# Where split weights and normed inputs begin in SBUF: four places 32 bytes apart, and two

## Chip, cores, metric

One core of one Trainium2 chip. The metric is the device time of one execution in microseconds (us), the median of several executions. Matmuls run on TensorE (PE), weight loads on the same engine's load path (PEld), and casts, sums and products on VectorE (DVE), ScalarE (ACT) and GpSimd (POOL).

## The reference, cut to what matters

Two layers run over 256 latent tokens and 256 context tokens, each 1,024 wide. A layer is a normed and modulated input, one wide input projection split among three token mixers (neighbourhood attention, retention, pooling), gated merges, an output projection and a SwiGLU feed-forward part:

```python
hx_n = _modulate(_rms_norm(h, norm1_g[l]), mx[:, 0], mx[:, 1])
hc_n = _modulate(_rms_norm(hc, norm1_g[l]), mc[0], mc[1])
mix_x, mix_c = _token_mixers(hx_n, hc_n, w_in[l], ...)
h = h + mx[:, 2] * mix_x
f_x = _modulate(_rms_norm(h, norm2_g[l]), mx[:, 3], mx[:, 4])
h = h + mx[:, 5] * _swiglu(f_x, w_ffn_gate[l], w_ffn_up[l], w_ffn_down[l])
```

In layer 0 the context tokens go the same way; in layer 1 they are only read. All in float32.

## The kernel before, in words

Every float32 product of a weight matrix is made of three matmuls on values cut in two. A value is rounded to the matmul's reduced float32 type (the high part) and the rest is kept as the low part; `mm3` (lines 194 to 198) then adds high by high (line 196), low weight by high input (197) and high weight by low input (198) into one PSUM bank.

The weights come in 276 chunks of 128 x 1024 floats, 138 a layer. For each chunk `load_to` issues the DMA into one of three `raw` tiles (line 99, SP's queue). `prep_to` takes one of four tiles with the tag `hl`, of 2 x 1024 floats a partition, and ACT casts the high half (line 124); `prep_lo` has DVE subtract for the low half (line 113). `use` keeps this three chunks ahead of the matmuls. In the trace the weight tiles and the low parts of the normed input have the same name, `hl`: in a matmul's row, the name behind the comma (`pg<-hh,hl`) is the stationary operand, the one before it is the moving operand.

The normed input `hn` is 8 pairs of tiles of 512 floats a partition: `hh` (high) and `hl` (low), 256 context columns and 256 latent columns each. It is written by the norm's modulation (`Mod`, lines 301 to 338) and, as the merged mixer output, by `msplit`. `fm` (line 209) walks chunks with the weights stationary and the input moving: 512 columns in layer 0, mostly 256 (the latent half) in layer 1. `tokmajor` (line 232) has it the other way round: the weights move, 512 columns at a time, and `hn` is stationary. The feed-forward part's second matrix reads `fh` and `fl` (line 1141), and the branch projections `naq` and `br`.

The order of the work is written out by hand; the program sets waits by the tile ranges that an instruction reads and writes. `edge` (line 1054) joins two stages in layer 0 and from layer 0 to 1; `edge1` (line 1117) joins the output projection and the feed-forward part in layer 1.

Tiles stand one behind the other in the order in which they are first asked for. In the program before, the four weight tiles begin at bytes 27,456, 35,648, 43,840 and 52,032 of a partition, the sixteen `hn` tiles at 68,416 and every 2,048 bytes from there, and the eleven pairs of `fh` and `fl` at 127,232 and every 2,048 from there. Modulo 128 that is 64 for all weights, 64 for all of `hn`, and 0 for `fh` and `fl`, and 0 for `naq` and `br` too.

Of the kernel before, what the change touches and what calls it, by code (L numbers as in the profile page):

```python
# [9 lines left out]
F32R = mybir.dt.float32r  # L10
# [8 lines left out]
KT = 8  # L19
# [13 lines left out]
def hybrid_dit_kernel(ctx: ExitStack, tc: tile.TileContext, hT, wst, adaf, adan, vec_d,  # L33
# [5 lines left out]
    wp = ctx.enter_context(tc.tile_pool(name="wp", bufs=1))  # L39
    act = ctx.enter_context(tc.tile_pool(name="act", bufs=1))  # L40
# [6 lines left out]
    def pg():  # L47
        return pbank("g", 4)
# [13 lines left out]
    def tiny(n, name="tiny"):  # L62
# [10 lines left out]
    mods = [con.tile([128, 48, 2], F32, name=f"mods{l}") for l in range(2)]  # L73
    Ag = [con.tile([128, 2, 8, 2], F32, name=f"Ag{l}") for l in range(2)]
    lg = [con.tile([128, 20], F32, name=f"lg{l}") for l in range(2)]
    hn = [(act.tile([128, 512], F32R, name=f"hh{k}"), act.tile([128, 512], F32R, name=f"hl{k}"))
          for k in range(KT)]
    h = []

    def h_tiles():  # L80
# [14 lines left out]
    def load_to(i):  # L95
        while st["dma"] <= min(i, total - 1):
            j = st["dma"]
            raw_t[j] = raw_tile()
            nc.sync.dma_start(out=raw_t[j], in_=wst[j])
            st["dma"] += 1  # L100

    late = []

    def parts(j, t):
        if j >= KT:
            return [(t, slice(0, 1024))]
        return [(t[:, :, :896], slice(0, 896)), (st["w7"][:, :, j], slice(896, 1024))]

    def prep_lo(i=total):
        while late and late[0][0] <= i:  # L110
            j, r, t = late.pop(0)
            for a, b in parts(j, t):
                V.tensor_tensor(a[:, 1], r[:, b], a[:, 0].bitcast(F32), op=ALU.subtract)  # L113

    def prep_to(i, wait=False):
        if not wait:
            prep_lo(i)
        while st["prep"] <= min(i, total - 1):
            j = st["prep"]
            load_to(j)  # L120
            t = wp.tile([128, 2, 1024], F32R, name="hl", tag="hl", bufs=4)
            r = raw_t.pop(j)
            for a, b in parts(j, t):
                S.copy(a[:, 0], r[:, b])  # L124
            late.append((j, r, t))
            if not wait:
                prep_lo(i)
            hl_t[j] = t
            st["prep"] += 1
# [7 lines left out]
    def use(i):  # L137
        prep_to(min(i + 3, st["cap"]), st["lazy"])
        load_to(i + 5)
        flush()  # L140
# [12 lines left out]
    def tick():  # L153
        step(lanes["pool"])
        step(lanes["rope"])
        step(lanes["attn"])
        if st["half"] == 0:
            prep_lo()
            st["credit"] += st["rate"]
            while ada_q and st["credit"] >= 1:  # L160
                ada_q.pop(0)()
                st["credit"] -= 1
        st["half"] ^= 1
# [7 lines left out]
    def ada_drain(n=0):  # L171
        while len(ada_q) > n:
            ada_q.pop(0)()
# [30 lines left out]
    def mmk(o, bl, xs, cols, k):  # L204
        n = cols.stop - cols.start
        hi, lo = xs[k]
        mm3(o[:, :n], blk(*bl[k]), (hi[:, cols], lo[:, cols]), k == 0, k == len(bl) - 1)

    def fm(specs, xs, cols, group=1):
        n = cols.stop - cols.start  # L210
        per = 2 if n == 512 else 4
        i = cnt = 0
        while i < len(specs):
            grp = specs[i:i + (group if i == 0 else 1)]
            i += len(grp)
            outs = [pg() for _ in grp]
            for k in range(len(grp[0][0])):
                for (bl, ev), o in zip(grp, outs):
                    if cnt % per == 0:
                        tick()  # L220
                    cnt += 1
                    prep_to(bl[k][0])
                    if (bl[k][1] == 4 or k == len(bl) // 2) and o is outs[0]:
                        use(bl[k][0])
                    mmk(o, bl, xs, cols, k)
            for (bl, ev), o in zip(grp, outs):
                ev(o[:, :n])

    def chunk8(j):
        return [(j, b) for b in range(8)]  # L230
# [57 lines left out]
    def norm_bcast(y, tiles, R):  # L288
        for i, t in enumerate(tiles):
            TE.matmul(R[:, t * 128:(t + 1) * 128], y[:, i:i + 1].to_broadcast([128, 128]), ident,  # L290
                      start=True, stop=True)
        return R
# [824 lines left out]
    def edge1(accs, l2, j2):  # L1117
        y = norm_rstd(norm_sum(accs, (2, 3)), 2)
        m = Mod(l2, j2, norm_bcast(y, (2, 3), pT()), (1,))
        return m  # L1120

    def out_ffn(l, fp):
        both = l == 0
        cq = ALL if both else X
        streams = (0, 1) if both else (1,)
        base = l * NCH
        acc = new_acc()
        last = [None]

        def ev_res(col, k, fin):  # L1130
            def ev(o):
                for s in streams:
                    residual(l, col, k, s, o[:, (CTX, X)[s]] if both else o)
                if fin and k < KT - 2:
                    defer.append(lambda: sq_acc(acc, k, cq))
                elif fin:
                    flush()
                    last[0] = sq_acc(acc, k, cq)
            return ev

        hid = [(fp.tile([128, 512], F32R, name=f"fh{j}"), fp.tile([128, 512], F32R, name=f"fl{j}"))
               for j in range(HALF)]

        def gate(o, e, c):
            if "s" not in e:
                e["s"] = fp.tile([128, 512], F32, name="sg", tag="sg", bufs=3)
            S.activation(e["s"][:, c], o, AF.Silu)  # L1147

        def upp(o, e, c, j):
            V.tensor_tensor(e["s"][:, c], o, e["s"][:, c], op=ALU.mult)  # L1150
            split([t[:, c] for t in hid[j]], e["s"][:, c])

        def gu(half, j0):
            c0 = base + CF + half * 33
            specs = []
            for j in range(j0, HALF):
                e = {}
                specs += [(chunk8(c0 + 2 * j), lambda o, e=e: gate(o, e, cq)),
                          (chunk8(c0 + 2 * j + 1), lambda o, e=e, j=j: upp(o, e, cq, j))]
            return specs  # L1160

        sqrt_table()
        wo = [chunk8(base + CO + k) for k in range(KT)]
        specs = [(wo[k], ev_res(16, k, True)) for k in range(KT)]
        heads = [chunk8(base + CF + i) for i in range(3)]
        if both:
            ada_drain(16)
            st["rate"] = 0.0
            fm(specs[:6], hn, cq, group=2)
            outs = edge(wo[6:], hn, 16, l, acc, heads, l, 1)  # L1170
            ada_units(1, (0, 1), (0, 1))
            ada_units(1, (2, 3, 4, 5), (1,))
            st["rate"] = 0.6
            specs = gu(0, 0)
            for (_, ev), o in zip(specs, outs):
                ev(o)
            fm(specs[3:], hn, cq)
        else:
            ada_drain()
            st["cap"] = base + CF + 1  # L1180
            fm(specs, hn, cq, group=2)
            edge1((acc, last[0]), l, 1).go(8)
            st["cap"] = 10 ** 6
            fm(gu(0, 0), hn, cq, group=2)

        def down(half):
            c1 = base + CF + half * 33 + 22
            return [[(c1 + (11 * k + q) // 8, (11 * k + q) % 8) for q in range(11)] for k in range(KT)]

        if both:  # L1190
            ada_drain(64)
        fm([(bl, ev_res(40, k, False)) for k, bl in enumerate(down(0))], hid, cq)
        fm(gu(1, 0), hn, cq)
        sqrt_table()
        acc = new_acc()
        dn = down(1)
        specs = [(bl, ev_res(40, k, True)) for k, bl in enumerate(dn)]
        if both:
            st["rate"] = 0.0
            fm(specs[:6], hid, cq)  # L1200
            ada_drain(32)
            return edge(dn[6:], hid, 40, l, acc, [chunk8(NCH + CK + i) for i in range(3)], 1, 0)
        fm(specs[:7], hid, cq)
        yt = fp.tile([128, KT, 256], F32, name="yt")

        def scaled(k):
            S.activation(yt[:, k], h[k][:, X], AF.Copy, scale=vec[:, V_FG + k:V_FG + k + 1])

        for k in range(KT - 1):
            scaled(k)  # L1210
        fm(specs[7:], hid, cq)
        o = norm_sum((acc, last[0]), (2, 3))
        scaled(KT - 1)
        y = norm_rstd(o, 2)
        R = norm_bcast(y, (2, 3), pT())
        for k in range(KT):
            V.tensor_tensor(yt[:, k], yt[:, k], R[:, X], op=ALU.mult)
            if k % 2:
                nc.sync.dma_start(out=out[:, k - 1:k + 1], in_=yt[:, k - 1:k + 1])
# [130 lines left out]
```

## Time and profile before

| | before |
|---|---|
| median of 3 runs | 1366.77 us (1366.04 to 1368.06) |
| the profiled execution's own time | 1367.57 us |
| its span, first to last instruction | 1365.8 us |
| PE busy | 1326.2 us, 97% |
| DVE, ACT, POOL busy | 847.6, 580.7, 152.7 us |
| mean granted TensorE clock | 0.987 of full speed |

The span is what the trace shows; the profiled execution's time is 1.8 us longer than it. Matmuls are pipelined: the time that one takes from its start to its end is longer than the distance to the start of the next, so a matmul's cost in a dense stretch is read as the distance of starts.

### The profile page before, as it was taken

Reading aid. Unit: us, or ns where it says so; the run is one execution under the profiler, and the core shown is the slowest. Engines: PE = TensorE matmul, PEld = TensorE weight load, DVE = VectorE, ACT = ScalarE, POOL = GpSimd, SP = SyncE. Lnnn points to the kernel's source line nnn. Section 1 sums busy time; section 2 is a strip of 40 time slices with the busy share of each in tenths; the row PEclk is TensorE's granted clock in tenths of the full one; section 3 lists DMA queues with packets and bytes.
Section 4 is the critical chain, followed back from the end, with each engine's and each line's share of the span. In section 5 each row is a group of like instructions: output and inputs, shape, how many; then the busy total and the mean of one; then the engine's idle time right before and its main releaser. Section 6 shows DMA issues by size and latency. Waiting matters only on the chain.

```text
span 1365.8 us, 20012 instructions
## 1 busy us (share of the span) xinstructions
PE 1326.2 (97%) x7842; PEld 1151.9 (84%) x7842; DVE 847.6 (62%) x1454; ACT 580.7 (43%) x907; POOL 152.7 (11%) x213
## 2 busy tenths in 40 slices
PE   7999999899999999999999999999999999999997
PEld 5777777788888898888888888988889999899997
DVE  4566452877877666566565654676438877655554
ACT  4455555452232444232123232456466545643453
POOL 0034113211000010000000000232134200000000
PEclk8999999999999999999999999999999999999998
DMA  8433312343544514454445652143336665455552
GB/s 301 164 99 132 104 63 92 124 137 126 169 170 163 192 62 154 139 170 158 149 140 186 212 171 87 61 159 108 131 124 197 223 239 185 140 185 198 181 176 95
DMA packets 61150, 207.28 MB, mean 152 GB/s; under 512 B 6912, under 2 KB 11392, under 8 KB 60032
## 3 DMA queue, kind: packets, MB, share of 16 engines
q1 hardware_dynamic: 49392, 163.96, 35.8%
q10 hardware_dynamic: 11664, 42.04, 9.1%
q8 instruction: 62, 1.02, 0.3%
q14 instruction: 32, 0.26, 0.1%
HBM read 204.93 MB, written 1.05 MB: 151 GB/s over the span
## 4 chain that ended last, share of the span: by engine, by line
PE 89%; DVE 6%; ACT 3%; issue 1%; DMA 1%; POOL 0%; DVEq 0%; ACTq 0%; SPq 0%; POOLq 0%
PE pg L196 26%; PE pg L197 26%; PE pg L198 26%; PE po L941 1%; PE po L687 1%; PE pt L675 1%; DVE hl L113 1%; PE po L459 1%; PE ps L643 1%; PE ps L644 1%; DVE nakl L628 1%; DMA bm<-in_bias 1%; DVE rkl L876 0%; DVE naq L638 0%; DVE acc L494 0%
## 5 line engine op out<-in xcount | busy, mean ns | idle before, releaser
L196 PE MATMUL pg<-hh,hl 128*128 128x256 f32 (+1 forms) x1568 | 528.1, 337 | 2.5 <-ACT tmp L1000 1.4
L197 PE MATMUL pg<-hh,hl 128*128 128x256 f32 (+1 forms) x1568 | 522.9, 333 | 1.4 <-DVE hl L113 1.4
L198 PE MATMUL pg<-hl,hl 128*128 128x256 f32 (+1 forms) x1568 | 523.3, 334 | 0.6 <-POOL hl L326 0.5
L113 DVE TENSOR_TENSOR hl<-raw,hl 128x1024 fp32r<-128x1024 f32 (+1 forms) x276 | 341.4, 1241 | 172.2 <-ACT hl L124 166.9
L124 ACT CAST hl<-raw 128x1024 fp32r<-128x1024 f32 (+1 forms) x276 | 286.9, 1043 | 211.4 <-PE pg L198 112.3
L196 PEld LDWEIGHTS pg<-hh,hl 128*128 128x128 f32 x1568 | 299.7, 191 | 36.1 <-issue 3.8
L197 PEld LDWEIGHTS pg<-hh,hl 128*128 128x128 f32 x1568 | 299.6, 191 | 31.1 <-DVE hl L113 2.1
L198 PEld LDWEIGHTS pg<-hl,hl 128*128 128x128 f32 x1568 | 299.2, 191 | 30.6 <-POOL hl L326 1.4
L385 DVE CUSTOM_DVE_ANT_0 tmp<-ada,cb 128x1024 bf16<-128x1024 f32 x128 | 156.1, 1226 | 26.7 <-DMA ada<-in_adaf 17.3
L196 PE MATMUL pg<-fh,hl 128*128 128x256 f32 (+1 forms) x374 | 121.6, 325 | 0.0
L197 PE MATMUL pg<-fh,hl 128*128 128x256 f32 (+1 forms) x374 | 121.4, 325 | 0.0
L198 PE MATMUL pg<-fl,hl 128*128 128x256 f32 (+1 forms) x374 | 121.4, 325 | 0.0
L326 POOL TENSOR_TENSOR hl<-tmp,hh 128x256 fp32r<-128x256 f32 x20 | 14.8, 739 | 626.3 <-ACT hh L315 371.1
L298 ACT CAST fh<-sg 128x512 fp32r<-128x512 f32 (+1 forms) x44 | 22.6, 513 | 141.0 <-DVE sg L1150 141.0
L196 PEld LDWEIGHTS pg<-fh,hl 128*128 128x128 f32 x374 | 70.1, 187 | 7.2
L198 PEld LDWEIGHTS pg<-fl,hl 128*128 128x128 f32 x374 | 70.1, 187 | 7.2
L197 PEld LDWEIGHTS pg<-fh,hl 128*128 128x128 f32 x374 | 70.1, 188 | 7.1
L342 DVE SCALAR_TENSOR_TENSOR h<-pg,mods,h 128x256 f32<-128x256 f32 x72 | 32.7, 479 | 65.6 <-PE pg L198 65.4
L1150 DVE TENSOR_TENSOR sg<-pg,sg 128x512 f32<-128x512 f32 (+1 forms) x44 | 24.5, 556 | 51.2 <-PE pg L198 47.8
L1000 ACT ACTIVATE tmp<-pg 128x512 f32<-128x512 f32 (+1 forms) x48 | 23.5, 490 | 76.4 <-PE pg L198 75.2
L196 PE MATMUL pg<-hl,hh 128*128 128x512 f32 x128 | 50.8, 397 | 1.7 <-DVE nakl L628 1.7
L1147 ACT ACTIVATE sg<-pg 128x512 f32<-128x512 f32 (+1 forms) x44 | 21.6, 490 | 68.4 <-PE pg L198 68.4
(248 smaller groups left out, 1555.7 us busy)
## 6 DMA issues: line engine op xcount, KB each, us to landing
raw<-in_wst SPq DMA_DIRECT2D x276, 512.0 KB, 3.8
ada<-in_adaf ACTq DMA_DIRECT2D x80, 512.0 KB, 4.2
wn<-in_adan SPq DMA_DIRECT2D x8, 1024.0 KB, 7.4
h<-in_hT SPq DMA_DIRECT2D x16, 256.0 KB, 5.5
bm<-in_bias SPq DMA_DIRECT2D x32, 128.0 KB, 2.1
out<-yt SPq DMA_DIRECT2D x4, 256.0 KB, 3.2
cs<-in_rope SPq DMA_DIRECT2D x2, 256.0 KB, 3.1
pw<-in_pw SPq DMA_DIRECT2D x2, 256.0 KB, 3.8
```

The lines of the kernel that those rows point to most:

```text
L113: V.tensor_tensor(a[:, 1], r[:, b], a[:, 0].bitcast(F32), op=ALU.subtract)
L124: S.copy(a[:, 0], r[:, b])
L196: TE.matmul(o, wh, xh, start=a, stop=False)
L197: TE.matmul(o, wl, xh, start=False, stop=False)
L198: TE.matmul(o, wh, xl, start=False, stop=z)
L298: S.copy(d0, src)
L326: P.tensor_tensor(hn[k][1][:, c], t[:, c], hi, op=ALU.subtract)
L342: V.scalar_tensor_tensor(h[k][:, c], o, mods[l][:, col + k, s:s + 1], h[k][:, c], op0=ALU.mult, op1=ALU.add)
L385: V.tensor_tensor_reduce(out=tmp().bitcast(BF16), in0=tiles[n], in1=cb[s], scale=1.0, scalar=0.0, op0=ALU.mult, op1=ALU.add, accum_out=mod ...
L1000: S.activation(sg[f][:, cl], o, AF.Sigmoid)
L1147: S.activation(e["s"][:, c], o, AF.Silu)
L1150: V.tensor_tensor(e["s"][:, c], o, e["s"][:, c], op=ALU.mult)
```

## The change

The sixteen `hn` tiles become one tile of 16 x 512 + 32 floats, and `hn_at(off)` sets the sixteen views to begin `off` floats into it: 0 at first, 16 floats (64 bytes) from just ahead of the modulation that makes layer 1's mixer input, and 0 again from just ahead of the one that makes layer 1's feed-forward input. The four weight tiles become one tile of 4 x 2048 + 32 floats, in which chunk j takes the 2048 floats from `2048 * (j % 4) + 8 * (j % 4)`: each of the four places begins 32 bytes further into its 8,192 than the one before. This tile is asked for ahead of `raw`, and so stands ahead of it.

```diff
-    hn = [(act.tile([128, 512], F32R, name=f"hh{k}"), act.tile([128, 512], F32R, name=f"hl{k}"))
-          for k in range(KT)]
+    hnb = act.tile([128, 16 * 512 + 32], F32R, name="hn")
+    hn = []
+
+    def hn_at(off):
+        v = [hnb[:, 512 * i + off:512 * i + off + 512] for i in range(16)]
+        hn[:] = [(v[2 * k], v[2 * k + 1]) for k in range(KT)]
+
+    hn_at(0)
...
+    hlb = wp.tile([128, 4 * 2048 + 32], F32R, name="hl")
...
-            t = wp.tile([128, 2, 1024], F32R, name="hl", tag="hl", bufs=4)
+            t = hlb
+            o = 2048 * (j % 4) + 8 * (j % 4)
+            t = t[:, o:o + 2048].rearrange("p (a n) -> p a n", a=2)
...
             fm(specs, hn, cq, group=2)
+            hn_at(0)
             edge1((acc, last[0]), l, 1).go(8)
...
             ada_drain(32)
+            hn_at(16)
             return edge(dn[6:], hid, 40, l, acc, [chunk8(NCH + CK + i) for i in range(3)], 1, 0)
```

## Rows read from the trace of the kernel before

**Rows 1.** The page: busy time of PE; the chain's shares by engine.

```profile
PE 1326.2 (97%) x7842; PEld 1151.9 (84%) x7842; DVE 847.6 (62%) x1454; ACT 580.7 (43%) x907; POOL 152.7 (11%) x213
...
PE 89%; DVE 6%; ACT 3%; issue 1%; DMA 1%; POOL 0%; DVEq 0%; ACTq 0%; SPq 0%; POOLq 0%
```

**Rows 2.** Groups by line and form on PE: count, busy us, mean ns, idle before.

```profile
L196 PE MATMUL pg<-hh,hl 128*128 128x512 f32 x720 | 285.2, 396 | 0.0
...
L196 PE MATMUL pg<-hh,hl 128*128 128x256 f32 x848 | 242.9, 286 | 2.5 <-ACT tmp L1000 1.4 <-ACT hh L317 1.1
...
L196 PE MATMUL pg<-fh,hl 128*128 128x256 f32 x220 | 61.0, 277 | 0.0
...
L196 PE MATMUL pg<-fh,hl 128*128 128x512 f32 x154 | 60.7, 394 | 0.0
...
L196 PE MATMUL pg<-hl,hh 128*128 128x512 f32 x128 | 50.8, 397 | 1.7 <-DVE nakl L628 1.7
...
L196 PE MATMUL pg<-br,hl 128*128 128x512 f32 x64 | 25.4, 397 | 0.0
```

**Rows 3.** Windows on PE: stretch, length, busy (instructions), granted clock, DMA share, GB/s.

```profile
520.00:620.00 100.00, 100.00 (x443) 1.00 0.47 158
...
1170.00:1230.00 60.00, 60.00 (x503) 1.00 0.57 186
```

**Rows 4.** Timeline of PE (start us, us, instruction): ends of four dense stretches.

```profile
599.86 0.39 PE L198 MATMUL pg<-hl,hl 128*128 128x512 f32 x1
...
605.98 0.39 PE L198 MATMUL pg<-hl,hl 128*128 128x512 f32 x1
...
679.95 0.39 PE L196 MATMUL pg<-fh,hl 128*128 128x512 f32 x1
...
682.98 0.39 PE L197 MATMUL pg<-fh,hl 128*128 128x512 f32 x1
...
1199.73 0.28 PE L198 MATMUL pg<-hl,hl 128*128 128x256 f32 x1
...
1200.57 0.28 PE L196 MATMUL pg<-hh,hl 128*128 128x256 f32 x1
...
1249.78 0.28 PE L198 MATMUL pg<-fl,hl 128*128 128x256 f32 x1
...
1250.57 0.28 PE L196 MATMUL pg<-fh,hl 128*128 128x256 f32 x1
```

**Rows 5.** Groups by line and form on PE, from 864.5 to 1166 us.

```profile
L196 PE MATMUL pg<-hh,hl 128*128 128x256 f32 x416 | 119.4, 287 | 1.4 <-ACT tmp L1000 1.4
...
L197 PE MATMUL pg<-hh,hl 128*128 128x512 f32 x24 | 9.4, 392 | 0.0
```

**Rows 6.** Timeline of PE where two attention matmuls cut into a dense stretch.

```profile
102.06 0.39 PE L196 MATMUL pg<-hl,hh 128*128 128x512 f32 x1
...
102.52 0.39 PE L198 MATMUL pg<-hl,hh 128*128 128x512 f32 x1
102.74 0.39 PE L643 MATMUL ps<-nakd,naq 128*128 128x512 f32 x1
102.97 0.39 PE L644 MATMUL ps<-nakl,naq 128*128 128x512 f32 x1
...
104.12 0.39 PE L197 MATMUL pg<-hl,hl 128*128 128x512 f32 x1
```

**Rows 7.** The page's groups for the split's two steps, and PE's longest waits for it.

```profile
L113 DVE TENSOR_TENSOR hl<-raw,hl 128x1024 fp32r<-128x1024 f32 (+1 forms) x276 | 341.4, 1241 | 172.2 <-ACT hl L124 166.9
L124 ACT CAST hl<-raw 128x1024 fp32r<-128x1024 f32 (+1 forms) x276 | 286.9, 1043 | 211.4 <-PE pg L198 112.3
...
PE pg L197 <- DVE hl L113: 1.4, 3, 0.9
```

**Rows 8.** Timeline of the kernel's end: products into one tile, its DMAs out.

```profile
1358.95 2.73 DVE L1217 TENSOR_TENSOR yt<-yt,pt 128x256 f32<-128x256 f32 x8 [1.38 <-PE pt L290]
1359.79 2.59 SPq L1219 DMA_DIRECT2D out<-yt  x4
```

## The prediction, made before the changed kernel was run

> **What bounds the kernel now.** I read the page first: PE is busy for 97% of the span and the chain that ended last is 89% PE [rows 1]. So the time is the number of matmuls times the distance between their starts, and little else. The groups by line and form come next: lines 196 to 198 have one group each for every moving tile and width, nearly without idle time before them [rows 2]. The reader should see the counts there; each stands for one of the three lines of `mm3`. The windows then show that two dense stretches run at a granted clock of 1.00, the upper of its two levels (2.4 GHz) [rows 3], so what follows is not the clock. Last the timeline, for the distance of starts in four dense stretches [rows 4]:
>
> - `hn` moving, 512 columns: 599.86 to 605.98 us, 27 distances, 226.7 ns each.
> - `fh` moving, 512 columns: 679.95 to 682.98, 13 distances, 233.1 ns.
> - `hn` moving, 256 columns: 1199.73 to 1200.57, 7 distances, 120.0 ns.
> - `fh` moving, 256 columns: 1249.78 to 1250.57, 7 distances, 112.9 ns, with a rounding of some 1 ns.
>
> These four rates are the case. The weights come from the same four tiles in all of them; what differs is the moving tile. `hn` and the weights begin at 64 modulo 128, `fh` at 0. With `hn`, 512 columns are 6.5 ns cheaper than with `fh`, and 256 columns 7 ns dearer. So a start place does carry a price in this kernel, of about 6.7 ns a matmul, with a sign that turns with the width. If a column took one cycle of 2.4 GHz (an estimate: 213.3 and 106.7 ns for 512 and 256 columns), the excess would be 13 or 20 ns at the one width and 13 or 6.5 at the other: whole steps of 6.7.
>
> **What the change does, part by part.** Instructions: none are added or removed. ACT still casts 276 chunks, DVE still subtracts, SP still issues one load each, and the loads land in `raw` as before. The order on every queue stays.
>
> Places: the weight block is now asked for ahead of `raw`, so it takes byte 15,168 (27,456 less the three `raw` tiles of 4,096), and its four places begin at 64, 96, 0 and 32 modulo 128. `hn` moves to 68,544 (128 bytes on, for the 32 extra floats), which is 64 modulo 128 with offset 0 as before, and 0 with offset 16. Everything behind it moves by 256 bytes, so `fh`, `naq` and `br` stay at 0.
>
> Reading A, my forecast: the place of the moving operand sets the rate. That is how the rows differ, and in one more place: where a matmul on 64-placed data is followed by one whose weights are `naq`, at 0, its distance is 102.52 to 102.74, 0.22 us, no dearer than its neighbours [rows 6]. Then only these change:
>
> - `hn` at offset 16, 256 columns: 416 a line between 864.5 and 1166 us [rows 5], times three lines, 1,248 matmuls. From 120.0 to 113.3: 1,248 x 6.7 ns = -8.3 us.
> - `hn` at offset 16, 512 columns (keys and the retention's keys, which read the context too): 24 a line, 72 matmuls [rows 5], from 226.7 to 233.3: +0.5 us.
> - `tokmajor`, where the weights move: 128 a line, 384 matmuls [rows 2], a quarter at each place. At 64 nothing; at 0, 96 x 6.7 = +0.6 us; at 32 and 96 no row shows a price, so bounds: nothing, or one step of 6.7 on 192, +1.3 us. I take half, +0.6.
>
> Sum: -8.3 + 0.5 + 0.6 + 0.6 = -6.6 us.
>
> The 32-byte starts of the stationary operand are the largest unknown. Nothing in the trace of before loads weights for these matmuls from a place that is not a multiple of 64. The nearest rows are the two rates of each width [rows 4]. From below: half of all matmuls go from the dearer rate to the cheaper. From above: half go from the cheaper to the dearer. Beyond that by one further step of 6.7 ns on that half, either way. I take nothing, since by reading A the stationary place has no price, and keep both ends for the range.
>
> Rule and row: the Trainium skill's page "TensorE: Matmul & The Clock Gate", section "Part 2: What happens when you issue a matmul", says that the engine has two independent SBUF read ports, so that loading the next weights takes nothing from the running matmul. By that rule no place of either operand would matter, all groups would have one rate a width, and the sum would be 0 instead of -6.6 us. The rows disagree: 226.7 against 233.1 at 512 columns, 120.0 against 112.9 at 256.
>
> The split: ACT's cast takes 1,043 ns and DVE's subtraction 1,241 ns a chunk [rows 7], 2.3 us together, written to other start places than before. PE waited for DVE's low half three times, 1.4 us in all [rows 7], because the split runs three chunks ahead (24 matmuls of 120 to 227 ns each, 2.9 to 5.4 us a chunk). I cost a dearer write at nothing. If the cover were gone, a chunk in layer 1 would have to take over 2.9 us on DVE alone; 1,241 ns is far off.
>
> Waits: both blocks are now one tile each. The four weight ranges don't overlap (each begins 2,056 floats behind the last), so a cast waits for the last reader of the same place, as before for the tile of four chunks ago. `hn` at offset 16 overlaps its neighbour's old range by 64 bytes, but a modulation writes only after the sums over outputs that are made behind the last reads of the old `hn`. Cost nothing. If the program instead waited by whole tiles, every chunk would show its 2.3 us of split to PE: 276 x 2.3 = 630 us. Against that: DVE's 8 products into `yt` run without a break from 1358.95 while DMAs read other slices of the same tile from 1359.79 [rows 8].
>
> **The rivals.**
>
> B, the difference of the two places sets the rate. Before, it is 0 with `hn` and 64 with `fh`. After, every stage takes all four differences in turn, and the two that rows show average to 230.0 and 116.7 ns. 512 columns: 720 x 3 with `hn` and 384 in `tokmajor`, +3.3 ns each, +8.5 us; `fh` 154 x 3, -3.3, -1.5 us. 256 columns: 848 x 3 with `hn`, -8.5 us; `fh` 220 x 3, +2.2 us. The branch tiles have as many matmuls at either width and cancel (one row, x64, stands for them [rows 2]). Sum +0.7 us: no change, 1368. For it: from 102.06 to 104.12 nine distances take 2.06 us, 20 ns over nine of 226.7 [rows 6], and three of these matmuls have operands 64 apart: three steps of 6.7, where A has one. Against it: the step into `naq` itself is not dearer.
>
> C, a start at 32 or 96 takes the dearer rate at both widths: half of 2,544 matmuls of 512 columns with `hn` or moving weights, +6.7 ns, +8.5 us; half of some 950 at 256 columns with `fh` and the branch tiles, +3.2 us. Sum +11.7, 1379 us: slower. With A's gain beside it +5, still slower; it outweighs A from 2 ns on half of all 6,800 or so matmuls. One step beyond the dearer rate on that half would be 23 us more, 1402.
>
> D, a start at 32 or 96 takes the cheaper rate at both widths: half of 2,544 at 256 columns with `hn`, -8.5 us; half of some 750 at 512 with `fh` and the branches, -2.5. Sum -11, 1357 us; with one step beyond it, 1334.
>
> E, no place matters and the rates belong to the tiles for another reason, as the port rule above would have it: 1367 us.
>
> W, waits by whole tiles: about 2000 us.
>
> **How the numbers follow.** The sum goes against the profiled execution's own time: 1367.6 - 6.6 = 1361.0 us. The median shown lies 0.8 us lower, so I predict 1360.2. Chances: A 0.34, D 0.14, B and E together 0.23, C 0.27, W 0.02. What a measurement of this kernel can tell from no change is about 0.2%, 2.7 us. Faster: A and D, 0.48. Same: B and E, 0.23. Slower: C and W, 0.29. The range reaches from most of D to C's 1379: 1348 to 1380. Left out are the further steps on either side, and W, some 0.17. A's own range is 1357 to 1364 (its weakest term, the moving weights, and a tenth of the gain lost where a stretch of layer 1 is broken up by attention matmuls).
>
> **What would show it.** The profile after should have, in layer 1's gates and output projection, distances of 113 ns where there were 120; in layer 0's feed-forward stretch all at 226.7, whichever chunk; in layer 1's feed-forward part 120 still. Alternation from chunk to chunk, every 24 matmuls, would show that the stationary place counts, and refute A for B, C or D by the rates that the four chunks have. Waits of PE for `hl` beyond the 1.4 us would point to the split or to W. The prediction is wrong if weights at 32 or 96 have a rate that no row of before shows, or if the rate turns with a period other than 128 bytes, which these rows can't tell.

## The result: 1379.16 us, 0.9% slower, and the profile after

The kernel after takes 1379.16 us (1378.5 to 1382.1, three runs) beside 1366.77 us before: a ratio of 1.0090, 95% interval 1.0074 to 1.0106. The forecast was 1360.2. The profiled execution took 1378.5 us with a span of 1376.6; its granted clock is 0.987, as before.

The page after, the engines' busy time, which answers to [rows 1], and the split's two steps and PE's wait for it, which answer to [rows 7] (the wait with its total us, count and longest):

```profile
PE 1338.6 (97%) x7842; PEld 1153.7 (84%) x7842; DVE 848.4 (62%) x1454; ACT 580.6 (42%) x907; POOL 151.5 (11%) x213
...
L120 DVE TENSOR_TENSOR hl<-raw,hl 128x1024 fp32r<-128x1024 f32 (+1 forms) x276 | 341.6, 1242 | 176.9 <-ACT hl L133 174.9
L133 ACT CAST hl<-raw 128x1024 fp32r<-128x1024 f32 (+1 forms) x276 | 286.7, 1042 | 211.8 <-PE pg L207 110.8
...
PE pg L206 <- DVE hl L120: 0.8, 3, 0.3
```

As many instructions as before, DVE and ACT as busy as before, the subtraction and the cast as long to 1 ns, and PE waits for a low half three times, 0.8 us in all. Only PE is busier, 1338.6 us against 1326.2. So 12.4 us went into the matmuls themselves: into the distance between their starts.

Where along the span, the timeline tells. Three places in the kernel before (the first matmul of 256 columns at the end of layer 0's feed-forward part, the first down product of layer 1, the last product of all), and the same three after (lines 205 to 207 are 196 to 198 moved on):

```profile
849.35 0.28 PE L196 MATMUL pg<-fh,hl 128*128 128x256 f32 x1
...
1231.17 0.29 PE L196 MATMUL pg<-fh,hl 128*128 128x256 f32 x1
...
1354.28 0.28 PE L198 MATMUL pg<-fl,hl 128*128 128x256 f32 x1
```

```profile
859.10 0.28 PE L205 MATMUL pg<-fh,hl 128*128 128x256 f32 x1
...
1240.55 0.28 PE L205 MATMUL pg<-fh,hl 128*128 128x256 f32 x1
...
1365.41 0.29 PE L207 MATMUL pg<-fl,hl 128*128 128x256 f32 x1
```

The kernel after is 9.75 us late at the first, 9.38 at the second, 11.13 at the third. Nearly all of the loss is in layer 0, where the matmuls have 512 columns. From the first place to the second lie layer 1's mixer, from which the forecast took 8.3 us, and the first gate and up projections: together they gave back 0.4.

The timeline of after in two dense stretches, the first matmul of each chunk (24 matmuls from one to the next): `hn` with 512 columns and `fh` with 256. They answer to [rows 4].

```profile
695.94 0.40 PE L205 MATMUL pg<-hn,hl 128*128 128x512 f32 x1
...
701.44 0.40 PE L205 MATMUL pg<-hn,hl 128*128 128x512 f32 x1
...
707.04 0.40 PE L205 MATMUL pg<-hn,hl 128*128 128x512 f32 x1
...
712.62 0.39 PE L205 MATMUL pg<-hn,hl 128*128 128x512 f32 x1
...
718.23 0.40 PE L205 MATMUL pg<-hn,hl 128*128 128x512 f32 x1
...
1243.28 0.28 PE L205 MATMUL pg<-fh,hl 128*128 128x256 f32 x1
...
1246.16 0.28 PE L205 MATMUL pg<-fh,hl 128*128 128x256 f32 x1
...
1249.01 0.28 PE L205 MATMUL pg<-fh,hl 128*128 128x256 f32 x1
...
1251.88 0.30 PE L205 MATMUL pg<-fh,hl 128*128 128x256 f32 x1
...
1254.64 0.28 PE L205 MATMUL pg<-fh,hl 128*128 128x256 f32 x1
```

With 512 columns four chunks take 5.50, 5.60, 5.58 and 5.61 us: 229, 233, 232.5 and 234 ns a matmul, 232.2 on the mean, where before had 226.7 in its dense stretch. With `fh` and 256 columns they take 2.88, 2.85, 2.87 and 2.76 us: 120, 119, 119.5 and 115 ns, where before had 112.9. The rate turns from chunk to chunk, which the prediction named as what would refute reading A.

The windows of after, `hn` with 512 columns and `hn` at its first place with 256 (the columns are those of [rows 3], with the busy time of PE, PEld, DVE, ACT and POOL ahead of the clock):

```profile
700.00:800.00 100.00, 100.00 (x432) 80.90 (x432) 57.52 (x81) 28.29 (x36) 0.00 (x0) 1.00 0.55 184
...
1275.00:1325.00 50.00, 50.00 (x424) 50.00 (x423) 28.55 (x36) 23.83 (x36) 0.00 (x0) 1.00 0.54 186
```

The granted clock stands at 1.00, its upper level, in both: the clock is not the cause. 424 matmuls in 50 us, of which two overlap the ends, are 118.5 ns each at the second, where before had 120.0.

### The profile page after: what moved, and what is told of

It reads as the page before. It is cut to its first block, busy times and chain, and to the rows that moved or that the text cites. A ratio compares the mean times of both kernels' runs of the same rounds, so it can differ in the third digit from the quotient of the medians.

```text
span 1376.6 us, 20011 instructions
## 1 busy us (share of the span) xinstructions
PE 1338.6 (97%) x7842; PEld 1153.7 (84%) x7842; DVE 848.4 (62%) x1454; ACT 580.6 (42%) x907; POOL 151.5 (11%) x213
## 4 chain that ended last, share of the span: by engine, by line
PE 93%; DVE 3%; ACT 2%; issue 1%; DMA 0%; SPq 0%; POOL 0%; ACTq 0%; DVEq 0%; POOLq 0%
PE pg L205 28%; PE pg L206 28%; PE pg L207 28%; PE po L950 1%; PE po L696 1%; PE pt L684 1%; PE po L468 1%; PE ps L653 1%; PE ps L652 1%; DVE hl L120 1%; DMA h<-in_hT 0%; PE pg L789 0%; ACT hl L133 0%; ACT hn L326 0%; PE ps L922 0%
## 5 line engine op out<-in xcount | busy, mean ns | idle before, releaser
L205 PE MATMUL pg<-hn,hl 128*128 128x256 f32 (+1 forms) x1568 | 530.1, 338 | 2.5 <-ACT tmp L1009 1.4
L206 PE MATMUL pg<-hn,hl 128*128 128x256 f32 (+1 forms) x1568 | 524.3, 334 | 0.8 <-DVE hl L120 0.8
L207 PE MATMUL pg<-hn,hl 128*128 128x256 f32 (+1 forms) x1568 | 524.3, 334 | 0.5 <-POOL hn L335 0.4
L205 PEld LDWEIGHTS pg<-hn,hl 128*128 128x128 f32 x1568 | 297.1, 189 | 39.6 <-issue 3.6
L206 PEld LDWEIGHTS pg<-hn,hl 128*128 128x128 f32 x1568 | 297.1, 189 | 33.8 <-DVE hl L120 1.5
L207 PEld LDWEIGHTS pg<-hn,hl 128*128 128x128 f32 x1568 | 296.8, 189 | 33.5 <-POOL hn L335 1.3
L335 POOL TENSOR_TENSOR hn<-tmp,hn 128x256 fp32r<-128x256 f32 x20 | 14.8, 738 | 634.4 <-ACT hn L324 372.6
L205 PE MATMUL pg<-hl,hn 128*128 128x512 f32 x128 | 51.3, 401 | 1.7 <-DVE nakl L637 1.7
```

The source lines that it names most:

```text
L205: TE.matmul(o, wh, xh, start=a, stop=False)
L206: TE.matmul(o, wl, xh, start=False, stop=False)
L207: TE.matmul(o, wh, xl, start=False, stop=z)
L335: P.tensor_tensor(hn[k][1][:, c], t[:, c], hi, op=ALU.subtract)
```

## The experiments

**The theories.** In what follows, the distance is one of addresses: the start of the weights less the start of the moving operand, modulo 256 bytes. The time from the start of one matmul to that of the next is given in ns, as the matmul's rate. From the start places that the prediction and the list of tiles give: before, it is 0 with `hn` and 64 with the hidden tiles `fh`, in all chunks. After, the weights stand at 64, 96, 128 and 160 modulo 256, `hn` at 192 (its first place) and 0 (its second), `fh` at 0; so it is 128, 160, 192 and 224 with `hn` at its first place, and 64, 96, 128 and 160 with `hn` at its second and with `fh`.

- Theory 1: this distance sets the rate.
- Theory 2: starts 32 bytes off a 64-byte step are dear (rival C).
- Theory 3: the moving operand's place alone counts (reading A, which takes it modulo 128).
- Theory 4: merging the tiles costs the time by itself.

Each edit below is against the kernel after. Times stand beside those of before on the same chip.

**One place.** The merged tiles stay, the places go back.

```
-    hnb = act.tile([128, 16 * 512 + 32], F32R, name="hn")
+    hnb = act.tile([128, 16 * 512 + 96], F32R, name="hn")
...
-    hn_at(0)
+    hn_at(32)
...
-            o = 2048 * (j % 4) + 8 * (j % 4)
+            o = 2048 * (j % 4)
...
-            hn_at(0)
...
-            hn_at(16)
```

> The two large tiles of the change stay, but every weight chunk begins at the same place in its 8,192 bytes and the normed input has one place, so that each stationary operand starts as far from its moving operand, counted modulo 256 bytes, as in the kernel before: 0 bytes for the normed input, 64 for the FFN's hidden tiles. Theory 1 (the rate of the matmuls follows the distance between the start of the weights and the start of the moving operand, modulo 256): all four rates of [rows 4] come back, 226.7 and 233.1 ns at 512 columns, 120.0 and 112.9 at 256, and the time is that of before, 1,365 to 1,369 us. Theory 4 (merging sixteen and four tiles into one each, with the order of writes and waits that follows, costs the time): the distances of the kernel after stay, and so does most of its 12 us: 1,375 to 1,380 us.

1367.69 us, ratio 0.9992 (0.9982 to 1.0001). Its window from 700 to 800 us has 443 matmuls where after has 432; 100 us by 226.7 ns are 441. Merging costs nothing: theory 4 falls, and what the change costs, the places cost.

**Weights at one place, `hn` at two.**

```
-            o = 2048 * (j % 4) + 8 * (j % 4)
+            o = 2048 * (j % 4)
```

> The normed input has its two places as in the change; the weights have one, so no start is 32 bytes off a 64-byte step. Theory 1 (distance of the two starts modulo 256): normed input at its first place 128 bytes apart, at its second 64. Layer 0, 512 columns: 232.4 ns in every chunk (as after shows for its first of four places) where before has 226.7; layer-1 mixer at 256 columns 113.3 in every chunk where before has 120.0; layer-1 FFN 118.7; the hidden tiles as before. Sum against before: 2,160 x 5.7 ns = +12.3, about 1,240 x -6.7 = -8.3, about 1,290 x -1.3 = -1.7, and +1.6 for the token-major products: +4 us, 1,369 to 1,373 us. Theory 2 (starts 32 bytes off a 64-byte step cost, as rival C of the prediction has it): none is left, so nothing above before: 1,367 us or less. Theory 3 (the moving operand's place alone, reading A): layer 0 stays at 226.7, the layer-1 mixer goes to 113, about 1,360 us.

1372.78 us, ratio 1.0035 (1.0022 to 1.0049), +4.2 us where theory 1 said +4. Its window, the first product of 256 columns at the end of layer 0's feed-forward part, and a stretch of 48 matmuls of layer 1's mixer (the last line is the first matmul behind them):

```profile
700.00:800.00 100.00, 100.00 (x432) 81.08 (x431) 57.50 (x81) 28.30 (x36) 0.00 (x0) 1.00 0.57 182
...
858.17 0.28 PE L205 MATMUL pg<-fh,hl 128*128 128x256 f32 x1
...
1128.02 0.28 PE L205 MATMUL pg<-hn,hl 128*128 128x256 f32 x1
...
1133.46 0.28 PE L205 MATMUL pg<-br,hl 128*128 128x256 f32 x1
```

432 matmuls in 100 us, as in after, though no start is 32 bytes off: theory 2 falls. And `hn` stands at 64 modulo 128 here as it did before, with the weights at one place as before, and yet takes 232 ns where it took 226.7: reading A falls, and the period is not 128 bytes. That the place of the moving operand counts alone, but modulo 256, this run does not exclude; the next one does. At 858.17 us this kernel is 8.82 us behind the kernel before, where after is 9.75 behind: nearly all of layer 0's loss is here with the weights at one place. It comes from the 128 bytes by which the padding moved `hn`. The mixer's stretch takes 5.44 us, 113.3 ns each, as distance 64 should.

**Four places, `hn` moved to suit.** The weights keep the change's places; `hn` goes 128 bytes on, to distances of 0, 32, 64 and 96.

```
-    hnb = act.tile([128, 16 * 512 + 32], F32R, name="hn")
+    hnb = act.tile([128, 16 * 512 + 64], F32R, name="hn")
...
-    hn_at(0)
+    hn_at(32)
...
-            hn_at(0)
...
-            hn_at(16)
```

> The weights keep the change's four places 32 bytes apart; the normed input has one place throughout, so that the distances to it are 0, 32, 64 and 96 bytes in turn, and to the hidden tiles 192, 224, 0 and 32. Theory 1 (distance modulo 256): with 512 columns the first of four chunks takes 226.7 ns, the third and fourth 233.3; with 256 columns the first 120.0, the third 113.3, the fourth 120.0; the second, at 32 bytes, was not seen before and lies between 226.7 and 233.3, and 113 and 120. Hidden tiles: 229, 233, 226.7, unknown at 512, and 118, 118, 120, unknown at 256. Against after: 2,160 x -0.3 to -2.0 ns, 2,540 x -1.6 to +0.1 ns: 0 to -8 us, 1,371 to 1,379 us. Theory 2 (starts 32 bytes off a 64-byte step cost): the second and fourth of four chunks dear, the first and third cheap, in both widths the same chunks. Theory 3 (the moving operand's place alone): no alternation from chunk to chunk.

1378.39 us, ratio 1.0070 (1.0055 to 1.0085). The timeline, four chunks of `hn` with 512 columns and four with 256:

```profile
687.63 0.40 PE L205 MATMUL pg<-hn,hl 128*128 128x512 f32 x1
...
693.23 0.40 PE L205 MATMUL pg<-hn,hl 128*128 128x512 f32 x1
...
698.82 0.39 PE L205 MATMUL pg<-hn,hl 128*128 128x512 f32 x1
...
704.44 0.39 PE L205 MATMUL pg<-hn,hl 128*128 128x512 f32 x1
...
709.91 0.39 PE L205 MATMUL pg<-hn,hl 128*128 128x512 f32 x1
...
1273.59 0.28 PE L205 MATMUL pg<-hn,hl 128*128 128x256 f32 x1
...
1276.45 0.28 PE L205 MATMUL pg<-hn,hl 128*128 128x256 f32 x1
...
1279.29 0.28 PE L205 MATMUL pg<-hn,hl 128*128 128x256 f32 x1
...
1282.12 0.28 PE L205 MATMUL pg<-hn,hl 128*128 128x256 f32 x1
...
1284.93 0.28 PE L205 MATMUL pg<-hn,hl 128*128 128x256 f32 x1
```

At 512 columns the distances 32, 64, 96 and 0 take 233, 233, 234 and 228 ns: theory 1 to 1.3 ns. `hn` begins at one place in all four, so its place alone, modulo whatever number, does not set the rate: theory 3 falls altogether. At 256 columns the distances 0, 32, 64 and 96 take 119, 118, 118 and 117 ns, where 120, a new value, 113.3 and 120 were expected: here the theory gives the size only to some 5 ns. The last experiment, which finds 113.3 and 117.7 ns at distance 64, accounts for the third value, not for the fourth: at 256 columns, where the distance turns from chunk to chunk, it does not settle the rate alone.

**Two distances, chosen.** One place for the weights; distance 0 for `hn` and the hidden tiles of layer 0 (512 columns), 64 throughout layer 1 (256 columns).

```
-    hnb = act.tile([128, 16 * 512 + 32], F32R, name="hn")
+    hnb = act.tile([128, 16 * 512 + 64], F32R, name="hn")
...
-    hlb = wp.tile([128, 4 * 2048 + 32], F32R, name="hl")
+    hlb = wp.tile([128, 4 * 2048], F32R, name="hl")
...
-            o = 2048 * (j % 4) + 8 * (j % 4)
+            o = 2048 * (j % 4)
...
-            hn_at(0)
...
-            hn_at(16)
+            hn_at(48)
...
         with tc.tile_pool(name="ff0", bufs=1) as fp:
+            P.memset(fp.tile([128, 16], F32, name="pad"), 0.0)
```

> One place for the weights; the moving operands placed so that with 512 columns the two starts are 0 bytes apart modulo 256 (the normed input and the hidden tiles of layer 0) and in layer 1, at 256 columns, 64 bytes apart. Theory 1: 512 columns at 226.7 ns for the hidden tiles too (462 x -6.4 ns = -3.0 us against before), 256 columns at 113.3 for the normed input of layer 1 (about 2,286 x -6.7 = -15.2), some +1.8 for the 256-column products with the hidden tiles of layer 0 and the token-major products of layer 1: -16.5 us, 1,348 to 1,354 us. Theory 3 (the moving operand's place alone) expects the same of this kernel. Theory 2 (only starts 32 bytes off cost): no difference to before, 1,367 us.

1355.56 us, ratio 0.9923 (0.9891 to 0.9956): faster than both kernels, though short of the 1,348 to 1,354 expected, and its six times spread from 1350.0 to 1363.9. Its windows, `hn` and `fh` with 512 columns, `hn` and `fh` with 256:

```profile
700.00:800.00 100.00, 100.00 (x443) 82.81 (x442) 59.72 (x85) 29.19 (x37) 0.00 (x0) 1.00 0.60 196
640.00:690.00 50.00, 50.00 (x223) 41.38 (x222) 27.78 (x46) 9.96 (x10) 0.00 (x0) 1.00 0.47 152
1275.00:1325.00 50.00, 50.00 (x444) 50.00 (x443) 30.14 (x39) 25.95 (x38) 0.00 (x0) 1.00 0.58 193
```

443, 223 and 444 matmuls; after has 432 and 424 in the first and third, and 216 in the second. These are the rates of distances 0 and 64: the hidden tiles of layer 0 now run like `hn`, and `hn` of layer 1 as `fh` did.

**One column 128 times.** After, with the second FFN half's gate and up projections fed from one column of each weight block.

```
     def blk(j, b):
         t = hl_t[j]
+        if st.get("one"):
+            return [t[:, i, b * 128:b * 128 + 1].to_broadcast([128, 128]) for i in range(2)]
         return t[:, 0, b * 128:(b + 1) * 128], t[:, 1, b * 128:(b + 1) * 128]
...
+        st["one"] = True
         fm(gu(1, 0), hn, cq)
+        st["one"] = False
```

> The kernel after, in which the gate and up projections of the second FFN half (528 matmuls of 512 columns in layer 0, 528 of 256 in layer 1) take as stationary operand the first column of their block 128 times over; the rest of each block's values is left out of the result. The weight loads stay, as many and as wide, but they read one address per partition instead of 512 bytes. Theory 1a (the excess comes from the reads of the weight load beside the reads of the moving operand): the distances no longer turn from chunk to chunk with the four places, one value in all four, and it lies below the 229 to 233 ns and 118 to 120 ns of after; between 213.5 and 227, for 528 matmuls 1 to 10 us less in layer 0, up to 4 in layer 1. Theory 1b (the distance of the two starts acts in another way, so that how much the load reads doesn't matter): 232, 233, 229 and 233 ns in turn as in after, the same time. The first half's gate and up projections keep their turning distances under both.

1377.32 us in one run, 1367.65 before (after took 1379.16 beside 1366.77). The timeline, four chunks of those projections at either width, the same places in turn as in after:

```profile
696.34 0.40 PE L205 MATMUL pg<-hn,hl 128*128 128x512 f32 x1
...
701.90 0.40 PE L205 MATMUL pg<-hn,hl 128*128 128x512 f32 x1
...
707.46 0.40 PE L205 MATMUL pg<-hn,hl 128*128 128x512 f32 x1
...
713.02 0.40 PE L205 MATMUL pg<-hn,hl 128*128 128x512 f32 x1
...
718.58 0.40 PE L205 MATMUL pg<-hn,hl 128*128 128x512 f32 x1
...
1276.10 0.28 PE L205 MATMUL pg<-hn,hl 128*128 128x256 f32 x1
...
1278.82 0.28 PE L205 MATMUL pg<-hn,hl 128*128 128x256 f32 x1
...
1281.54 0.28 PE L205 MATMUL pg<-hn,hl 128*128 128x256 f32 x1
...
1284.26 0.28 PE L205 MATMUL pg<-hn,hl 128*128 128x256 f32 x1
...
1286.97 0.28 PE L205 MATMUL pg<-hn,hl 128*128 128x256 f32 x1
```

The turning is gone: 5.56 us, 231.7 ns, in every chunk of 512 columns, and 2.72 us, 113.3 ns, in every chunk of 256. ACT and DVE write the halves to the four places as before, so their writes are not what turns the rate: the place acts through the addresses that the weight load reads (theory 1a). That these reads get in the way of the moving operand's is the likeliest reading; no run shows where the two would meet. What 1a said of the size is half wrong: 256 columns fell to the lowest rate seen, but 512 columns stayed at 231.7, far above 227. What makes up that excess at 512 columns when one address is read is open.

**Steps of 256 bytes.** Four places again, 256 bytes apart.

```
-    hnb = act.tile([128, 16 * 512 + 32], F32R, name="hn")
+    hnb = act.tile([128, 16 * 512 + 64], F32R, name="hn")
...
-    hlb = wp.tile([128, 4 * 2048 + 32], F32R, name="hl")
+    hlb = wp.tile([128, 4 * 2048 + 256], F32R, name="hl")
...
-            o = 2048 * (j % 4) + 8 * (j % 4)
+            o = 2048 * (j % 4) + 64 * (j % 4)
...
-            hn_at(16)
+            hn_at(0)
```

> Four places for the weights in turn, 256 bytes apart instead of 32; the normed input at one place, 0 bytes apart modulo 256, the hidden tiles 64, as in the kernel before. Theory 1 with a period of 256 bytes: all four places are one, the distances of before in every chunk (226.7, 233.1, 120.0, 112.9 ns) and its time, 1,365 to 1,370 us. With a period of 512 or 1,024 bytes: the distances turn with the place in every second or each of four chunks, and the time lies above before, up to the 1,379 of after. Theory that four places in turn cost by themselves: 1,379 us.

1368.03 us, ratio 1.0005 (0.9994 to 1.0017), with 443 matmuls in the window from 700 to 800 us. Four places in turn cost nothing when they are equal modulo 256. With the kernel of weights at one place, where 128 bytes more cost 5.7 ns a matmul, the period is 256 bytes.

**Steps of 16 bytes**, in two kernels (`8 * (j % 4)` becomes `4 * (j % 4)`, the block of `hn` grows, and the arguments of `hn_at` change; in the second kernel `hn` keeps one place, so the two later calls go).

> Four places for the weights 16 bytes apart, and places of the moving operands chosen so that one run shows many distances. 512 columns: normed input 0, 16, 32, 48; hidden tiles 64, 80, 96, 112. 256 columns: layer-1 mixer 64 to 112, layer-1 FFN 0 to 48 in one part and 128 to 176 in the other as the code places them. Theory 1 at 0, 64, 96, 128 and 160 has values from the kernels so far: 226.7, 233.3, 233.3 at 512 columns (0, 64, 96), 120, 113.3 or 117.7, 120, 118.7, 119.7 at 256 (0, 64, 96, 128, 160); 32 bytes as in the shifted kernel, 233 and about 117. New are the steps of 16 between. If the reads are of lines of 32 bytes or more, the distances at 16, 48 and 80 equal one of their neighbours; if of 16 or less, they may stand by themselves. The time lies between before and after, 1,367 to 1,380 us.

> Weights at four places 16 bytes apart, the normed input 192, 208, 224 and 240 bytes from them at both widths, the hidden tiles 0, 16, 32 and 48. Theory 1: 229 and 233.3 ns at 192 and 224 with 512 columns, 118 and 118 with 256, as in after; hidden tiles of layer 0: 226.7 at 0, 227 at 16, 233 at 32 and 48, as the normed input had them in the run with steps of 16; hidden tiles of layer 1: 120 at 0. New are 208 and 240. No distance of 256 columns below 113.3 is expected. If the tiles had rates of their own, and not the distance, the hidden tiles would stay at 233.3 in layer 0.

1377.79 and 1373.10 us, one run each. The first one's timeline, one chunk with 512 columns at 16 bytes, behind hidden tiles at 64, and then four at 0, 16, 32 and 48 bytes:

```profile
687.21 0.39 PE L205 MATMUL pg<-hn,hl 128*128 128x512 f32 x1
...
692.81 0.40 PE L205 MATMUL pg<-hn,hl 128*128 128x512 f32 x1
...
704.00 0.40 PE L205 MATMUL pg<-hn,hl 128*128 128x512 f32 x1
...
709.46 0.39 PE L205 MATMUL pg<-hn,hl 128*128 128x512 f32 x1
...
714.91 0.39 PE L205 MATMUL pg<-hn,hl 128*128 128x512 f32 x1
...
720.50 0.40 PE L205 MATMUL pg<-hn,hl 128*128 128x512 f32 x1
...
726.10 0.40 PE L205 MATMUL pg<-hn,hl 128*128 128x512 f32 x1
```

The last four take 227.5, 227, 233 and 233 ns: 16 bytes apart is as good as 0, 32 is dear. But the first chunk, at 16 bytes too, takes 5.60 us, 233.3 ns. It stands behind matmuls of 233 ns, the other behind matmuls of 227: in the dense stretches a run at 16 bytes kept the rate that it came with, so the distance alone does not settle it. In the second kernel the hidden tiles of layer 0 had these distances, and the window from 640 to 690 us holds 219 matmuls where after has 216: the mean of 227, 227, 233 and 233 ns gives 217, and two that overlap its ends. The tiles have no rate of their own. Of the two distances that were new, 208 took 232.1 ns (a chunk from 707.62 to 713.19 us) and 240 took 229.6 (718.78 to 724.29). With 256 columns distance 64 had the lowest mean in these two kernels, 114.5 ns, and no other lay below 116. In what units the operands are read stays open.

**The chosen distances in layer 0's mixer too**: as the kernel with two distances, and one line more.

```
         with tc.tile_pool(name="mx0", bufs=1) as mp:
+            P.memset(mp.tile([128, 16], F32, name="pad"), 0.0)
```

> As the kernel with two distances, and in the mixer of layer 0 the attention's outputs and the convolution's branches stand 0 bytes from the weights too (282 matmuls of 512 columns). Theory 1: 282 x -6.4 ns = -1.8 us against that kernel, 1,349 to 1,362 us with its spread; the lowest of the runs near 1,348. In the traces the runs of 256-column matmuls at 64 bytes hold either 113.3 or 117.7 ns from one pause to the next, as in that kernel, and which of the two a long run takes sets the spread (2,286 x 4.4 ns = 10 us between all of the one and all of the other).

1354.60 us (1350.4 to 1362.9), ratio 0.9905 (0.9871 to 0.9939): the lowest median here, 1 us below the kernel with two distances, which is far less than either one's spread. PE is busy for 1307.9 us, 18.3 less than before.

**Why these two kernels spread: two more traces of the first of them.** Nothing is edited.

> The kernel with two distances once more, for a second trace of it. In the first trace, whose execution took 1,352.5 us, some 2,200 of the 256-column matmuls at 64 bytes stood 113 or 114 ns apart and some 820 of them 117 to 119; other executions took 1,350.0 to 1,363.9. Theory 5 (two steady cycles at this one distance, 113.3 and 117.7 ns, which a run of matmuls enters after a pause and keeps): the time of this execution differs from 1,352.5 by 4.4 ns for each matmul that changes its cycle, so 2 us for some 450 of them, all else the same within 2 us. Rival: the spread comes from pauses or the clock: the two rates hold the same share, and PE's idle time or the granted clock differs by what the time does.

> As the run before it, a third trace of the same kernel, with the same expectations of both theories.

1353.34 and 1355.94 us. One window of each trace over the same work in layer 1's mixer, first the one then the other:

```profile
1106.00:1132.00 26.00, 26.00 (x232) 26.00 (x232) 20.89 (x34) 13.01 (x21) 0.00 (x0) 1.00 0.68 237
```

```profile
1107.00:1133.00 26.00, 26.00 (x223) 26.00 (x222) 20.22 (x33) 12.24 (x21) 0.00 (x0) 1.00 0.70 227
```

232 and 223 matmuls in 26 us, at the same clock and without a wait: about 113 ns in the one and 117.7 in the other, for the same program and distance. So theory 5 has its two cycles. Beyond that it is only partly borne out. The first trace has 2,204 such matmuls of 113 to 115 ns, the second 2,330, the third 2,041. The 289 that the third has less than the second are worth 1.3 us; but the second has more of them than the first, and its execution is still 0.8 us longer. Nearly half of the 2.6 us between the second and the third comes from elsewhere (the slower one is 1.2 us behind at the end of layer 0 already), and no trace fell on an execution above 1356.

## Why the prediction was wrong

**What bounds the kernel**: right. The times between PE's starts are the kernel's time, and a change of them shows in full.

**Split, waits, moves**: right at nothing. The cast and the subtraction are as long as before, PE waits no longer for them, and one place with the merged tiles gives the time of before.

**Reading A, the step that failed.** It took the four rates as prices of the moving operand's place, counted modulo 128, and so put two things at nothing that both cost: the 128 bytes by which the padding moves `hn`, and the four places of the weights. The rates were prices of a difference, modulo 256; the weights had one place in all four rows, so these could not tell the one from the other. What spoke for A against B was one step into `naq`, 0.22 us in [rows 6], where a line is rounded to 10 ns and the price was 6.7. The 128 bytes alone make `hn` with 512 columns take 232 ns (432 matmuls in 100 us with the weights at one place) and put layer 0 8.82 us behind; the four places then keep layer 1 from most of its gain.

The size: with `hn` and 512 columns, 2,160 matmuls of layer 0 went from 226.7 to 232.2 ns in the dense stretches. Taken matmul by matmul over both traces (every start that follows directly on another) it is 4.8 ns on the mean, +10.0 us: in the mixer part of them (some 170 of 530 from 90 to 335 us) took over 229 ns before the change too. All four places are dear there, so this alone is more than the bound that took half of the matmuls to the dearer rate (+8.5).

**-8.3 us from `hn` at its second place**: refuted. The timeline of after has a stretch of 48 of these in the mixer between two lines:

```profile
1130.71 0.30 PE L205 MATMUL pg<-hn,hl 128*128 128x256 f32 x1
...
1136.36 0.28 PE L205 MATMUL pg<-br,hl 128*128 128x256 f32 x1
```

5.65 us, 117.7 ns each; two others like it took 119.3 and 117.4. Over all 1,248 the matmuls became 1.7 ns cheaper: -2.0 us. The 113.3 was there to be had: the kernel with the weights at one place shows it.

**The rest**, by the same pairs of matmuls. `hn` at its first place with 256 columns, 1,296 matmuls: -2.0 us. `fh` with 256 columns, 660, from 113.5 to 118.3 ns: +3.1. `fh` with 512 columns: 233 ns still, nothing. Branch tiles with 256 columns: +0.8. The products with moving weights, +0.6 in the forecast: +1.3. The 72 of layer 1 with 512 columns, +0.5 in the forecast: +0.3. Sum with the two above: +11.5 us; the span grew by 10.8 (1365.8 to 1376.6), and the pauses between the stretches are some 0.7 us shorter in all.

**The port rule** of the Trainium skill (page "TensorE: Matmul & The Clock Gate", section "Part 2: What happens when you issue a matmul") would have given 0. The trace differs: the same matmul takes 226.7 or 233 ns by where weights and moving operand begin. That a column read 128 times over ends the turning shows that what the load reads is not without effect on the matmuls here.

**The rivals.** B had the right quantity, the difference, and failed in its period (128 bytes; it is 256) and in its prices: it averaged the two differences that rows showed, 230.0 and 116.7, where after's four give 232.2 and about 118.2. The rows of before could not tell this; that the period might be another was named as a way to be wrong. C's time, 1379, came true for another reason, and it is by luck that the stated range, whose upper end was set by C, holds the 1379.16 us: the chunks with weights at 64, which did not move, slowed as well, and without any 32-byte start the time is still 1372.78, 4.2 us above before, with layer 0's loss nearly whole. The 32 floats of padding pushed `hn` 128 bytes on, to a place that the prediction held to be equal, because it counted modulo 128. The four places cost the other 8 us or so, most of it in layer 1: what they took away there are the 113.3 ns that the weights at one place give.

## What to carry to other kernels

Where PE is busy for nearly all of a span, tabulate the times between matmul starts against the start of the weights less the start of the moving operand, before moving any tile; padding moves every tile behind it. In this kernel 0 bytes modulo 256 was best for 512 columns (16 did as well in some chunks) and 64 for 256, and setting both took some 1% off. Rows in which one operand never moves can't tell that operand's price from a price of the difference: an edit that moves one and holds the other still can.

## What the runs showed of the hardware

- The rate depends on where the weights begin beside the moving operand, with a period of 256 bytes: 226.7 to 234 ns with 512 columns, 113.3 to 120 with 256, at the upper clock. It is no single penalty: 0 bytes is cheapest at 512 columns and among the dearest at 256. Within a chunk a matmul's own weights and the next ones have the same place modulo 256, so which of the two counts was not told apart.
- At some distances two steady rates exist, and a run of matmuls keeps the one that it has: 113.3 and 117.7 ns at 64 bytes with 256 columns, 226.7 and 233 at 16 bytes with 512. What chooses at 64 is open, and so is whether this is all of the 14 us that the kernel with two distances spreads over.
- Reading one column for all of a weight block takes away the effect of the place, and leaves 113.3 ns with 256 columns and 231.7 with 512.
